# A one-core decoder step: page numbers kept for two loads, and a few orders at its seams

## The chip, the cores and the metric

The kernel is one program on one core of a Trainium2 chip. The metric is the device time in microseconds. The times of before are three runs with a median of 1844.89 us (1842.65 to 1846.63). One more execution was taken by the hardware profiler; every row of the profile below is of that one.

Engines are named as in the profile: PE is the matrix engine (PEld its weight loads), DVE the vector engine, ACT the scalar engine, POOL the general one, and SP the engine whose queue (SPq) issues almost all DMAs here. Each takes its instructions in the order of its own queue.

## The reference, cut to what matters

One layer of a decoder for two groups of requests: a prompt of 1024 tokens and 8 decode requests with 4 new tokens each. The change touches three pieces.

- The prompt's causal attention: 8 heads, scores of queries and keys, exponential, values (`masked_attend` in blocks of 128).
- The decode requests' attention over a paged cache. For each request `pages = page_table[b]` picks 32 pages of 128 tokens; a page holds latents (`cache_ckv`, 256 wide) and rope keys (`cache_kpe`, 32 wide). Keys come from the latents, `k = rms_norm(concat(c @ w_uk, pe))` per head, and `o = softmax(q k) v` runs over 4096 cached tokens and the new ones.
- Keys and values of 256 memory tokens: `k = rms_norm(hm @ w_mk)`, `v = hm @ w_mv`, with `hm = rms_norm(mem)`. They do not depend on the two attentions.

After these come an output projection, memory attention and a gated convolution network; they are left as they are.

## The kernel before

Every product of 32-bit numbers is three matmuls on a high and a low part of each operand (`mm3`, L180; the matmul itself is L185). A high part is cast by ACT or POOL (L197, L201), a low part is left to DVE (L198, L204). The stages in order of time: `phase1`, `phase2a` (the prompt's attention, about 200 to 400 us), `phase2b` (the decode requests, about 400 to 900 us, with `mem_kv` at its end), then `mixed`, `out_proj`, `mem_attention`, `ffn`.

**Who sets the order.** Inside `manual_schedule(engines=...)` the engines named keep the order of the Python program. All other engines, and all of them outside, are ordered by a planner that plays the program forward in modelled time and takes, on each engine, the earliest instruction in the program that it holds to be ready. So in `phase2a` and most of `phase2b` the orders of PE, ACT, DVE and POOL are written by hand and SP's is planned; at the end of `phase2b` only SP's is by hand and the others' are planned. `behind(a, b)` puts instruction a behind b on their engine without a semaphore.

**`phase2a`.** `order` lists 16 units (head h, half G of the queries). A unit has steps; in each step t the loop does: transposes of probabilities `u["T"]` (L993, copied out by ACT L995), pending exponentials `u["e"]` (ACT L985), scores of a coming unit `u["a"]` (PE L185 into tile s of two buffers, drained by DVE L976 and L980 into pr with the row maximum, L982), values `u["V"]` (L1008), and then whatever `extra[t]` holds: key and query transposes of a coming head (`preps`, L946), norms of the keys (`norm`, DVE L922), projected values (`v1`), sums of weights (`weight_sums`, SP L828 and L840, POOL L836 to L839), and one step of each running generator. `jobs[t]` says which scores of which unit fall into step t. One generator is `mix`, with `mix_steps`: four squares with row sums (ACT L1610), a root (DVE), four scalings (ACT L1616), four groups of transposes (PE L1624, copied by DVE L1625). Another is `sample`, which ends in `pages_ahead`: the page table and the latents of quads 0 to 2.

**`phase2b`.** A quad is 4 pages of a request: 8 quads each, 64 in all. `quad_load` reads the four page numbers into registers of SP (L1302, `values_load`), and issues for each page one DMA of transposed latents into tile cT (L1315, three buffers) or of rows into tile ck (L1319, 15 buffers), or both; each call reads the numbers anew. `quad_rot` makes rotated rope keys krq (POOL L1332 to L1334) from cT; `quad_prep` splits cT into ch (ACT L1343) and cl (half on POOL, half on DVE, L1347); `quad_sums` takes squares of the rope keys from ck (ACT L1355, DVE L1356). The steps n count pairs of blocks, two pairs to a quad; `pair_score` does rope scores of the next quad on odd n (PE L1362, copied by ACT L1365) and 24 matmuls (L185) into tile s (two buffers) and s2, whose squares ACT takes (L1384, L1387) and DVE reduces (L1390). Values `quad_pv` (L1460, L1462) follow 20 steps later, after a request's `batch_softmax`, whose parts are numbered r. In part 11 PE spreads a maximum over the partitions (L1448), ACT copies it (L1450), DVE or POOL subtracts it (L1451); the last part is the exponential (ACT L1453).

The loads of the first quads do not all have the same place: cT of quads 0 to 2 is loaded in `phase2a`, of 3 and 4 at n = -1 and 1, ck of quads 0 to 4 at n = 1, 2, 3, 3, 5, and from quad 5 on `quad_load` does both at n = 2Q - 6.

**The end of `phase2b`.** The last request's softmax and values run beside `mem_kv`. Its value products come in four parts, `values(0)`, `(2)`, `(4)`, `(6)`, each 12 matmuls into two accumulators (L185, tile v). Then ACT scales each accumulator into tile vf, which has one buffer (L1592), and issues its DMA to the output (L1593). The norm of the keys uses diag (DVE L1582) and PE L1583.

Of the kernel before, what the change touches and what calls it, by code (L numbers as in the profile page):

```python
# [13 lines left out]
P = 128  # L14
# [140 lines left out]
class Net:  # L155
# [23 lines left out]
    def mm3(self, out, a, b, first=True, last=True):  # L179

        seq = []
        for (ah, al), (bh, bl) in zip(a, b):
            seq += [(ah, bh), (ah, bl), (al, bh)]
        for i, (l, r) in enumerate(seq):
            self.nc.tensor.matmul(out, l, r, start=first and i == 0, stop=last and i == len(seq) - 1)  # L185

    def behind(self, a, b):

# [466 lines left out]
    def phase2a(self):  # L655
# [67 lines left out]

        for n in range(1, len(units)):
            places = {(1, 0): (0, 0, 1, 2), (0, 1): (-1, -1, 0, 1), (0, 0): (0, 0, 1, 1), (1, 1): (0, 1, 1, 2)}
            at = places[order[n - 1][1], order[n][1]] if n > 1 else (0, 0, 1, 1)
            for e in range(4):
                jobs[starts[n - 1] + at[e]].append((units[n], e))

# [3 lines left out]
        for h in range(2, 8):  # L733
            b = 7 * (h - 1)
            put(preps[h], {3: (9, 10, 12, 13), 5: (28, 29, 34, 35), 6: (32, 33, 41, 42), 7: (39, 38, 44, 46)}.get(h, (b, b + 1, b + 3, b + 4)))
        extra[1][:0] = preps[0][2:]
        spread(late[0][0], 11, 21)
        spread(late[1][0], 14, 24)
        spread(late[0][1], 22, 27)
        spread(late[1][1], 25, 30)  # L740
        spread(late[2][0], 24, 30)
        sums = [(i, z) for i in (NK, NK + 1, *range(NK)) for z in range(2)]
        times = (0, 1, 3, 4, 5, 7, 8, 9, 11, 12, 14, 15, 16, 25, 26, 27, 29, 30, 36, 37, 39, 40, 41, 43, 44, 46)
        for t, x in zip(times, sums):
            extra[t].append(lambda x=x: self.weight_sums(half(), *x))

# [17 lines left out]
        with tc.manual_schedule(engines={E.PE, E.Activation, E.DVE, E.Pool}):  # L764
            for f in preps[0][0], preps[0][1], v1[0], preps[1][0], preps[1][1]:
                f()
            for e in range(4):
                units[0]["a"](e)
                if e:
                    units[0]["e"](e - 1)  # L770
                    if e % 2:
                        v1[e // 2 + 1]()
            units[0]["e"](3)
            for f in norm[:2]:
                f()
            v1[3]()
            extra[0][:0] = norm[2:]
            steps, outs, pend, V = [], {}, [], []
            self.lows = []
            t = 0  # L780
            for n, u in enumerate(units):
                for k, banks in enumerate(u["steps"]):
                    self.flush()
                    for b in banks:
                        u["T"](b)
                    for f in outs.pop(t, []):
                        f()
                    for f in pend:
                        f()
                    pend = []  # L790
                    for w, e in jobs[t]:
                        w["a"](e)
                        pend.append(lambda w=w, e=e: w["e"](e))
                    self.flush()
                    for f in V:
                        f()
                    V = [lambda u=u, b=b: u["V"](b) for b in banks]
                    if k == len(u["steps"]) - 1:
                        outs.setdefault(t + 2, []).append(u["copy"])
                        outs.setdefault(t + 3, []).append(u["out"])  # L800
                        if order[n] == (7, 0):
                            outs[t + 3].append(lambda: steps.append(mix()))
                    for f in extra[t]:
                        f()
                    t += 1
                    if t == 32:
                        steps.append(sample())
                    steps = [x for x in steps if next(x, 0) is None]
            self.flush()
            self.lows = None  # L810
            for fs in [V] + [outs[t] for t in sorted(outs)] + [[]] * 4:
# [306 lines left out]
    def pages_ahead(self):  # L1118

        nc, I = self.nc, self.I  # L1120
        pc = self.pc3 = self.open("p3c", side="right")
        self.pages = self.t(pc, [1, NB * NPG], I32, "pages")
        nc.sync.dma_start(self.pages, I["pages"])
        self.cosT, self.sinT = (self.t(pc, [P, 8, P], F32, x) for x in ("cosT", "sinT"))
        nc.sync.dma_start(self.cosT, I["c_cosT"])
        nc.sync.dma_start(self.sinT, I["c_sinT"])
        yield
        self.quads = {Q: self.quad_load(None, Q) for Q in range(3)}
        yield
        nc.vector.tensor_scalar(self.cosT, self.cosT, self.col("gk_rep"), None, ALU.mult)  # L1130
        yield
        nc.vector.tensor_scalar(self.sinT, self.sinT, self.col("gk_perm"), None, ALU.mult)


    def phase2b(self):
# [19 lines left out]
        def at(n, pos, f, *a):  # L1155
            ev.setdefault((n, pos), []).append(lambda: f(*a))
# [45 lines left out]
                    at(n + k, pos, f)  # L1202
        E = mybir.EngineType

        raws = []

        def steps(n0, n1):
            for n in range(n0, n1):
                Q, v = n // 2, n - 16 - LAG
                if n >= 4 and n % 2 == 0 and Q + AHEAD < NB * 8:  # L1210
                    quads[Q + AHEAD] = self.quad_load(p, Q + AHEAD)
                for k, dst, src in ((2, b4, self.b_dram), (16, self.fold4, I["c_fold4"]), (64, wuv, I["w_uv"])):
                    if n == k:
# [19 lines left out]
                run(n, 1)  # L1233
# [60 lines left out]
        for w, q in ((self.w2h, self.qah), (self.w2l, self.qal)):  # L1294
            nc.scalar.copy(w[:, :, d], q[:, :, b].rearrange("p k h t -> p k (h t)"))

    def quad_load(self, p, Q, d=None):

        nc, I = self.nc, self.I
        new = d is None  # L1300
        d = d or {}
        ld, rvs = nc.values_load_multi_w_load_instructions(  # L1302
            self.pages[0:1, Q * 4 : Q * 4 + 4], engines=[mybir.EngineType.SP], min_val=0, max_val=319
        )
# [1 line left out]
        if len(self.page_dma) >= 5:  # L1306
            for x in ld:
                self.tc.add_manual_dep(
                    x.ins, self.page_dma[-5].ins.name,
                    mybir.DependencyInfo(mybir.DependencyClass.NoSync, mybir.DependencyReason.DATA), reason="registers",  # L1310
                )
        dmas = []
        if new:
            cT = d["cT"] = self.t(self.pc3, [P, 4, 320], F32, "cT", 3)
# [79 lines left out]
    def batch_softmax(self, p, pp, s, r, final):  # L1394
# [50 lines left out]
            nc.vector.tensor_scalar(s["dg"], self.ident[:32, :32], mm, None, ALU.mult)  # L1445
        elif r == 11:
            bc = self.t(pp, [P, 512], F32, "m", 1)[:, :32]
            nc.tensor.matmul(bc, self.ones[:32], s["dg"], start=True, stop=True)  # L1448
            s["bc"] = self.t(p, [P, 32], F32, "bc", 2)
            nc.scalar.copy(s["bc"], bc)  # L1450
            (nc.vector if final else nc.gpsimd).tensor_tensor(S, S, s["bc"].unsqueeze(1).broadcast_to([P, 33, 32]), ALU.subtract)  # L1451
        else:
            nc.scalar.activation(S, S, AF.Exp, scale=SCALE)  # L1453

    def quad_pv(self, pp, Q, d, s):

# [47 lines left out]
    def mem_kv(self, raws, wk0):  # L1504
# [44 lines left out]
        def values(k):  # L1549
            wh, wl = (x.rearrange("p k n -> p (k n)").rearrange("p (k n) -> p k n", k=2) for x in self.stream(I["w_mv"][k // 2], 8))  # L1550
            for i in range(2):
                t = slice(i * P, i * P + P)
                self.mm3(av[i], [tuple(x[:, t] for x in xs[k + e]) for e in range(2)],
                         [(wh[:, e], wl[:, e]) for e in range(2)], first=k == 0, last=k == 6)

        values(0)
        yield
# [31 lines left out]
        values(6)  # L1589
        for i in range(2):  # L1590
            vf = self.t(p, [P, 512], F32, "vf")
            nc.scalar.activation(vf, av[i], AF.Copy, scale=rt[:, i : i + 1])  # L1592
            nc.scalar.dma_start(O["o_mv"][i * P : i * P + P], vf)  # L1593
        self.close("pskv")
        self.close("pkv")
# [840 lines left out]
```

## Time and profile before

| | us |
|---|---|
| median of three runs | 1844.89 |
| the profiled execution | 1842.78 |
| its span, first to last instruction | 1841.1 |
| PE busy in it | 1807.4 |
| POOL, ACT, DVE busy | 699.7, 925.4, 1350.2 |

The span leaves out 1.7 us around it. PE's idle time is the span less its busy time; an idle gap carries in brackets what ended it. In a list of waits the numbers are: us in total, times, longest. In a table of windows each engine has its busy us and in brackets its instructions; PEclk is the granted clock of PE as a share of full speed. A slowed PE counts as busy.

### The profile page before, as it was taken

The numbers are of one execution on the slowest core, as the hardware profiler recorded it, in microseconds if no ns is written. First come the engines' busy times: TensorE is split into PE (matmuls) and PEld (weight loads), VectorE is DVE, ScalarE is ACT, GpSimd is POOL, SyncE is SP. The second block draws the span as 40 slices with busy tenths as digits, with TensorE's granted clock in tenths as the row PEclk, the third lists the DMA queues.
The fourth block names the chain that finished last, engine by engine and source line by source line (L and its number), as shares of the span: only waits on it lengthen the run. The fifth ranks groups of instructions, "written<-read, shape, count | busy, mean of one in ns | idle before, by whom it ended". The sixth has DMA issues, their size and how long they took to land.

```text
span 1841.1 us, 39335 instructions
## 1 busy us (share of the span) xinstructions
PE 1807.4 (98%) x14222; PEld 1705.8 (93%) x14222; DVE 1350.2 (73%) x2805; ACT 925.4 (50%) x1916; POOL 699.7 (38%) x852
## 2 busy tenths in 40 slices
PE   9999999999999999999899999999999999999999
PEld 8999777679999999998799979999999999999999
DVE  7855767656778766776545666998888888878664
ACT  7435676766656555555433556533333333444442
POOL 1021555533544454454123110377766777400000
PEclk9999999999999999999999999999999999999999
DMA  8101363557766666654555255322222222495242
GB/s 320 47 25 65 104 205 105 185 174 201 226 188 195 188 182 184 184 166 144 158 154 178 73 179 161 107 82 70 94 82 70 73 80 76 142 328 171 80 152 77
DMA packets 153188, 261.19 MB, mean 142 GB/s; under 512 B 20897, under 2 KB 97538, under 8 KB 152994
## 3 DMA queue, kind: packets, MB, share of 16 engines
q1 hardware_dynamic: 152130, 257.63, 45.3%
q8 instruction: 112, 1.84, 0.4%
q10 hardware_dynamic: 864, 1.05, 0.2%
q14 instruction: 82, 0.67, 0.1%
HBM read 212.79 MB, written 45.82 MB: 140 GB/s over the span
## 4 chain that ended last, share of the span: by engine, by line
PE 71%; issue 5%; DVE 4%; SPq 3%; DMA 2%; POOL 2%; ACT 2%; POOLq 0%; DVEq 0%; ACTq 0%
PE s L185 14%; PE d L185 12%; PE b L185 8%; PE F L185 7%; PE X L185 7%; PE E L185 7%; PE A L185 3%; PE y L185 3%; SPq L1315 2%; PE o L1008 2%; PE tp L993 1%; PE tp L185 1%; PE o L1462 1%; DMA cT<-cT 1%; POOL cl L1347 1%
## 5 line engine op out<-in xcount | busy, mean ns | idle before, releaser
L185 PE MATMUL s<-w2h,ch 128*128 128x288 f32 (+1 forms) x1024 | 304.4, 297 | 0.5 <-ACT S L1365 0.5
L185 PE MATMUL s<-w2h,cl 128*128 128x288 f32 (+1 forms) x1024 | 296.3, 289 | 2.3 <-POOL cl L1347 2.3
L185 PE MATMUL s<-w2l,ch 128*128 128x288 f32 (+1 forms) x1024 | 295.2, 288 | 0.0
L185 PEld LDWEIGHTS s<-w2h,ch 128*128 128x128 f32 x1024 | 193.2, 189 | 9.0 <-issue 2.5
L185 PEld LDWEIGHTS s<-w2h,cl 128*128 128x128 f32 x1024 | 192.9, 188 | 4.1 <-POOL cl L1347 3.9
L185 PEld LDWEIGHTS s<-w2l,ch 128*128 128x128 f32 x1024 | 193.4, 189 | 0.0
L1390 DVE TENSOR_REDUCE ss<-sq 128x16 f32<-128x1024 f32 x128 | 155.4, 1214 | 33.0 <-ACT sq L1387 32.7
L1347 POOL TENSOR_TENSOR cl<-cT,ch 128x512 fp32r<-128x512 f32 x64 | 82.9, 1295 | 120.4 <-ACT ch L1343 115.4
L1387 ACT ACTIVATE sq<-s 128x512 f32<-128x512 f32 x128 | 76.7, 599 | 88.3 <-PE s L185 88.2
L1384 ACT ACTIVATE sq<-s 128x512 f32<-128x512 f32 x128 | 76.9, 601 | 73.3 <-PE s L185 70.9
L197 ACT CAST a<-brb 128x528 fp32r<-128x528 f32 x77 | 49.0, 636 | 109.5 <-PE d L185 105.8
L185 PE MATMUL d<-a,w 128*128 128x264 f32 x768 | 95.2, 284 | 0.0
L185 PEld LDWEIGHTS d<-a,w 128*128 128x128 f32 x768 | 94.3, 188 | 0.0
L198 DVE TENSOR_TENSOR a<-brb,a 128x528 fp32r<-128x528 f32 x77 | 54.4, 707 | 52.8 <-ACT a L197 52.7
L2072 POOL TENSOR_TENSOR lo<-s,hi 128x1024 fp32r<-128x1024 f32 x20 | 64.0, 3200 | 45.7 <-ACT hi L2071 45.7
L185 PE MATMUL mm<-whi,xh 128*128 128x256 f32 (+3 forms) x272 | 77.1, 285 | 0.0
L185 PE MATMUL mm<-wlo,xh 128*128 128x256 f32 (+3 forms) x272 | 76.9, 285 | 0.1
L185 PE MATMUL mm<-whi,xl 128*128 128x256 f32 (+3 forms) x272 | 76.9, 286 | 0.0
L2127 ACT COPY a<-A 128x264 f32<-128x264 f32 x43 | 16.2, 376 | 120.5 <-PE A L185 114.2
L1386 DVE TENSOR_TENSOR S<-s,S 128x64 f32<-128x64 f32 x128 | 28.1, 219 | 63.6 <-ACT sq L1384 63.6
L1343 ACT CAST ch<-cT 128x512 fp32r<-128x512 f32 x128 | 73.6, 628 | 2.0 <-DMA cT<-cT 1.3
L2193 POOL TENSOR_TENSOR cv<-cv,row 128x1056 f32<-128x1056 f32 x22 | 65.1, 2960 | 21.0 <-ACT cv L2192 21.0
(746 smaller groups left out, 6397.1 us busy)
## 6 DMA issues: line engine op xcount, KB each, us to landing
cT<-cT SPq DMA_DIRECT2D x256, 160.0 KB, 2.7
ck<-ck SPq DMA_DIRECT2D x256, 144.0 KB, 3.4
raw<-w_up SPq DMA_DIRECT2D x44, 512.0 KB, 3.6
wsumd<-wsum SPq DMA_DIRECT2D x26, 512.0 KB, 3.4
actd<-cv SPq DMA_DIRECT2D x44, 264.0 KB, 2.4
brb<-actd SPq DMA_DIRECT2D x44, 264.0 KB, 5.9
wsum<-w_down SPq DMA_DIRECT2D x22, 512.0 KB, 3.6
raw<-wsumd SPq DMA_DIRECT2D x20, 512.0 KB, 3.8
```

Of the source, the lines that this page charges most:

```text
L185: self.nc.tensor.matmul(out, l, r, start=first and i == 0, stop=last and i == len(seq) - 1)
L197: first = {"act": nc.scalar.copy, "pool": nc.gpsimd.tensor_copy, "dve": nc.vector.tensor_copy}[eng](hi, src)
L198: low = lambda: nc.vector.tensor_tensor(lo, src, hi, ALU.subtract)
L1008: nc.tensor.matmul(u["o"][g : g + 64, o : o + m * P], s["v"][:, j, h % 4], th[:, z * P : (z + m) * P], start=j == 0, stop=b == len(banks) - 1,
L1315: dmas.append([nc.sync.dma_start(cT[:, j], I["cT"][bass.ds(rv, 1)].rearrange("a p n -> (a p) n")) for j, rv in enumerate(rvs)])
L1343: nc.scalar.copy(d["h"][:, k], src[k])
L1347: (nc.vector if k else nc.gpsimd).tensor_tensor(d["l"][:, k], src[k], d["h"][:, k], ALU.subtract)
L1384: nc.scalar.activation(sq[:, 0], ps[:, :, n0 : n0 + 256], AF.Square)
L1387: nc.scalar.activation(sq[:, 1], pt.rearrange("p (e d) -> p e d", e=2), AF.Square)
L1390: yield lambda: nc.vector.tensor_reduce(s["ss"][:, g0 : g0 + 2].rearrange("p e (z h) -> p z e h", z=2), sq.rearrange("p z e (h d) -> p z e ...
L2072: eng.tensor_tensor(lo, src, hi, ALU.subtract)
L2193: nc.gpsimd.tensor_tensor(cv, cv, row, ALU.mult)
```

## The change

- `quad_pages` is split off from `quad_load`; page numbers that were read are kept in `rvs` and passed to the second load of the same quad. Those of quads 3 and 4 are read at the end of `pages_ahead`.
- In `phase2b` the first loads get other steps: cT of quads 5 to 7 at n = 3, 5, 7, ck of quads 0 to 7 at n = 1, 3, 4, 5, 6, 3, 8, 8; loads of both from quad 8 on. `quad_sums` of quads 0 to 4 moves to n = 6, 8, 10, 10, 11 (before 4, 6, 8, 7, 9).
- Tiles m, o and s2 are allocated before s, so that their places in PSUM (PE's output banks) are given in that order.
- In `phase2a`: v1's last part and the second half of head 0's transposes move from ahead of step 0 and from step 1 to steps 1 and 2; the third unit's scores move to steps 3, 3, 3, 4 (before 2, 2, 3, 4); the first two `weight_sums` move one step on; `mix` does one square in its first step and three in its second (before two and two).
- At the end: the first matmul of `values(6)` is put behind L1448 on PE, and the second vf behind the last exponential on ACT.

```diff
     def mm3(...):
+        returns its first matmul (head)
...
-            at = places[order[n - 1][1], order[n][1]] if n > 1 else (0, 0, 1, 1)
+            at = {1: (0, 0, 1, 1), 2: (0, 0, 0, 1)}.get(n) or places[order[n - 1][1], order[n][1]]
...
-        extra[1][:0] = preps[0][2:]
+        extra[2][:0] = preps[0][2:]
...
-        times = (0, 1, 3, 4, 5, 7, 8, 9, 11, 12, 14, 15, 16, 25, 26, 27, 29, 30, 36, 37, 39, 40, 41, 43, 44, 46)
+        times = (1, 2, 3, 4, 5, 7, 8, 9, 11, 12, 14, 15, 16, 25, 26, 27, 29, 30, 36, 37, 39, 40, 41, 43, 44, 46)
...
-                if k not in (0, 2, 8):
+                if k not in (1, 2, 8):
                     yield
...
-            v1[3]()
             extra[0][:0] = norm[2:]
+            extra[1][:0] = v1[3:]
...
         self.quads = {Q: self.quad_load(None, Q) for Q in range(3)}
+        self.rvs = {Q: self.quad_pages(Q) for Q in (3, 4)}
...
         ppt, pp = self.open("ps3t", space=PSUM), self.open("ps3", space=PSUM)
+        for tag in ("m", "o"):
+            self.t(ppt, [P, 512], F32, tag, 1)
+        self.t(pp, [P, 512], F32, "s2", 2)
...
-                if n >= 4 and n % 2 == 0 and Q + AHEAD < NB * 8:
+                if n >= 10 and n % 2 == 0 and Q + AHEAD < NB * 8:
                     quads[Q + AHEAD] = self.quad_load(p, Q + AHEAD)
...
-                    at(n + (6 if Q < 2 else 3), 0, self.quad_sums, Q + 1, quads[Q + 1], st[(Q + 1) // 8])
+                    at((6, 8, 10, 10, 11)[Q + 1] if Q < 4 else n + 3, 0, self.quad_sums, Q + 1, quads[Q + 1], st[(Q + 1) // 8])
...
-                if n in (-1, 1):
-                    quads[Q + 4] = self.quad_load(None, Q + 4)
-                for k in {1: (0,), 2: (1,), 3: (2, 3), 5: (4,)}.get(n, ()):
-                    self.quad_load(p, k, quads[k])
+                if n in (-1, 1, 3, 5, 7):
+                    k = Q + 4
+                    rvs[k] = rvs.get(k) or self.quad_pages(k)
+                    quads[k] = self.quad_load(None, k, None, rvs[k])
+                for k in {1: (0,), 3: (5, 1), 4: (2,), 5: (3,), 6: (4,), 8: (6, 7)}.get(n, ()):
+                    self.quad_load(p, k, quads[k], rvs.get(k))
...
-    def quad_load(self, p, Q, d=None):
+    def quad_load(self, p, Q, d=None, rvs=None):
+        rvs = rvs or self.quad_pages(Q)
...
-            nc.tensor.matmul(bc, self.ones[:32], s["dg"], start=True, stop=True)
+            self.spread = nc.tensor.matmul(bc, self.ones[:32], s["dg"], start=True, stop=True)
...
-            nc.scalar.activation(S, S, AF.Exp, scale=SCALE)
+            self.exp = nc.scalar.activation(S, S, AF.Exp, scale=SCALE)
...
+                if k == 6 and i == 0:
+                    self.behind(x, self.spread)
...
+            if i:
+                self.behind(x, self.exp)
```

More of the change, by code (lines that the diff above doesn't have):

```diff
@@ L184, in mm3 @@
         for i, (l, r) in enumerate(seq):
-            self.nc.tensor.matmul(out, l, r, start=first and i == 0, stop=last and i == len(seq) - 1)
+            x = self.nc.tensor.matmul(out, l, r, start=first and i == 0, stop=last and i == len(seq) - 1)
+            if i == 0:
+                head = x
+        return head
     def behind(self, a, b):
@@ L1203, in phase2b @@
         E = mybir.EngineType
-        raws = []
+        raws, rvs = [], self.rvs
         def steps(n0, n1):
@@ L1295, in batch_enter, with quad_pages @@
             nc.scalar.copy(w[:, :, d], q[:, :, b].rearrange("p k h t -> p k (h t)"))
-    def quad_load(self, p, Q, d=None):
-        nc, I = self.nc, self.I
-        new = d is None
-        d = d or {}
+    def quad_pages(self, Q):
+        nc = self.nc
         ld, rvs = nc.values_load_multi_w_load_instructions(
@@ L1311, in quad_load @@
                 )
+        return rvs
+    def quad_load(self, p, Q, d=None, rvs=None):
+        nc, I = self.nc, self.I
+        new = d is None
+        d = d or {}
+        rvs = rvs or self.quad_pages(Q)
         dmas = []
@@ L1552, in values @@
                 t = slice(i * P, i * P + P)
-                self.mm3(av[i], [tuple(x[:, t] for x in xs[k + e]) for e in range(2)],
-                         [(wh[:, e], wl[:, e]) for e in range(2)], first=k == 0, last=k == 6)
+                x = self.mm3(av[i], [tuple(x[:, t] for x in xs[k + e]) for e in range(2)],
+                             [(wh[:, e], wl[:, e]) for e in range(2)], first=k == 0, last=k == 6)
+                if k == 6 and i == 0:
+                    self.behind(x, self.spread)
         values(0)
@@ L1591, in mem_kv @@
             vf = self.t(p, [P, 512], F32, "vf")
-            nc.scalar.activation(vf, av[i], AF.Copy, scale=rt[:, i : i + 1])
+            x = nc.scalar.activation(vf, av[i], AF.Copy, scale=rt[:, i : i + 1])
+            if i:
+                self.behind(x, self.exp)
             nc.scalar.dma_start(O["o_mv"][i * P : i * P + P], vf)
```

## The prediction, made before the result was known

> **What bounds the kernel now.** I read the page first, then PE's list of waits, then the timelines around each wait.
>
> ```profile
> span 1841.1 us, 39335 instructions
> PE 1807.4 (98%) x14222; PEld 1705.8 (93%) x14222; DVE 1350.2 (73%) x2805; ACT 925.4 (50%) x1916; POOL 699.7 (38%) x852
> ```
>
> PE is idle for 33.7 us of the span. The change removes no matmul, so it can win only idle time and time at a lowered clock.
>
> ```profile
> PE o L1460 <- ACT S L1453: 5.3, 1, 5.3
> PE s L1362 <- POOL krq L1334: 5.1, 3, 2.3
> PE tp L946 <- DVE k L922: 1.8, 2, 1.1
> ```
>
> These three groups are 12.2 us, and all lie at places that the change edits: the last exponential, the first quads of `phase2b`, and head 0's keys at the opening of `phase2a`. A gap can cost more than itself. The table of windows (us; PE, PEld, DVE, ACT, POOL busy and instructions; granted clock; DMA share; GB/s) has these rows:
>
> ```profile
> 214.00:219.00 5.00, 4.98 (x17) 3.56 (x17) 2.68 (x10) 0.58 (x2) 2.21 (x4) 0.50 0.52 169
> 431.00:434.00 3.00, 1.58 (x12) 1.58 (x13) 1.03 (x2) 2.41 (x7) 2.54 (x4) 1.00 0.78 209
> 441.00:445.00 4.00, 3.73 (x18) 3.73 (x19) 2.81 (x4) 2.55 (x6) 1.45 (x2) 0.57 0.79 220
> 894.00:901.00 7.00, 6.51 (x71) 5.69 (x71) 0.02 (x1) 3.27 (x7) 0.00 (x0) 0.68 0.19 60
> ```
>
> After the 5.3 us gap the clock is 0.68 for 7 us: 2.2 us lost. At 441 it is 0.57 for 4 us: 1.7 us lost. At 431 it stays at 1.00.
>
> **The change, 1: page numbers and first loads.** PE's three waits for rope keys, what held POOL before the second and third, and SP's queue:
>
> ```profile
> 402.40 0.46 PE L1362 MATMUL s<-bd,krq 128*128 128x128 f32 x2 [1.41 <-POOL krq L1334]
> 432.42 0.49 PE L1362 MATMUL s<-bd,krq 128*128 128x128 f32 x2 [1.43 <-POOL krq L1334]
> 441.27 0.80 PE L1362 MATMUL s<-bd,krq 128*128 128x128 f32 x2 [2.29 <-POOL krq L1334]
> ```
>
> ```profile
> 430.96 0.46 POOL L1332 TENSOR_TENSOR krq<-cT,cosT 128x128 f32<-128x128 f32 x1 [5.78 <-DMA cT<-cT]
> 439.82 0.45 POOL L1332 TENSOR_TENSOR krq<-cT,cosT 128x128 f32<-128x128 f32 x1 [6.21 <-DMA cT<-cT]
> ```
>
> ```profile
> 414.95 8.60 SPq L1319 DMA_DIRECT2D ck<-ck  x12
> ...
> 425.25 1.92 SPq L1315 DMA_DIRECT2D cT<-cT  x4
> ...
> 434.64 2.23 SPq L1315 DMA_DIRECT2D cT<-cT  x4
> ...
> 446.34 2.33 SPq L1315 DMA_DIRECT2D cT<-cT  x4
> ```
>
> The latents of quads 5, 6 and 8 are issued at 425.25, 434.64 and 446.34. The first two were late: POOL stood idle for them, PE for POOL. SP was never idle there; its price is in the chain (start, us) and the landing times on the page:
>
> ```profile
> 406.12 6.05 PE s L185 x48
> ...
> 429.25 0.30 SPq L1302
> ...
> 430.78 0.32 SPq L1319
> ```
>
> ```profile
> cT<-cT SPq DMA_DIRECT2D x256, 160.0 KB, 2.7
> ck<-ck SPq DMA_DIRECT2D x256, 144.0 KB, 3.4
> ```
>
> One read of four page numbers takes 1.5 us (429.25 to 430.78), four issues about 2.1, and PE needs 3.1 us for a pair (6.05 for 48 matmuls, and the rope).
>
> Quad 5: before, SP did ahead of its latents two loads of latents, four of rows and seven reads. After, it does two, one, and two reads (the numbers of 3 and 4 are read in `phase2a`: 3 us more in SP's queue there, with only stores and loads of weight sums behind them, which no PE wait names). That is 3 x 2.1 + 5 x 1.5 = 13.8 us less, 411.5 for the issue. But the tile is that of quad 2, still read until 412.8:
>
> ```profile
> 402.17 0.69 DVE L1347 TENSOR_TENSOR cl<-cT,ch 128x512 fp32r<-128x512 f32 x1
> ...
> 411.79 1.02 DVE L1347 TENSOR_TENSOR cl<-cT,ch 128x512 fp32r<-128x512 f32 x1
> ```
>
> So the issue is at 412.8 to 414.9, landing at 417.5; PE asks for the keys at 431. Quad 6: two loads and four reads less, 10.3 us, of which 2.3 go to waits for tiles (1 us for quad 4's, 1.3 for quad 5's): issue at 426.6, landing 431.3, keys (1.4 us of POOL) 432.7; PE asks at 402.5 + 11 x 3.1 = 437. Quad 8: four reads less, 3.8 us net: issue 442.5, landing 447.3, keys 448.7; PE asks at 402.5 + 15 x 3.1 = 449. That is the thinnest cover, 0.3 us (1 us where the opening transposes come between). What is late next, if any, is here. The rows of quads 1 to 4 are now loaded 3 to 6 us later, and their `quad_sums` stand in ACT's queue ahead of the squares that free s. By the same count rows 3 land at 434 and are asked for at n = 10, 434: ACT waits some tenths, and s has two buffers, so PE feels a delay only beyond about one pair (3.1 us).
>
> Won: 1.43 + 2.29 + 1.7 of clock = **5.4 us**. Its ends: 0 if the latents stay where they were in SP's order, 5.4.
>
> [...] The row at 441, 0.57 right behind that gap, speaks for the gap as the cause, and the row at 431 for a bound between 1.43 and 2.29.
>
> **2: the first pair.** Allocating m, o and s2 first gives tile s other banks than those that `mix` copied out just before 402.40; if that copy, not the keys, ended the wait, PE starts up to 1.41 earlier. But the sixth matmul of the pair reads the half of cl that DVE ends at 402.86 (row above), 0.4 us before it runs now. I take **0.35**; the ends are 0 and 1.41.
>
> **3: mix.** ACT's second square stands ahead of an exponential that PE waits for:
>
> ```profile
> 388.84 0.63 ACT L1610 ACTIVATE k<-b_all 128x512 f32<-128x512 f32 x1
> ```
>
> ```profile
> 391.11 0.76 PE L993 MATMUL tp<-ident,pr 128*128 128x128 f32 x5 [1.09 <-ACT pr L985]
> ```
>
> It moves behind it: the gap shrinks by 0.7. The three squares then end when the second two did, and the copies behind them hold PE by 0.4. I take **0.3** (0 to 0.7).
>
> **4: the opening.** The waits for L922 are 1.12 and 0.65. Beside them:
>
> ```profile
> 205.76 0.33 PE L993 MATMUL tp<-ident,pr 128*128 128x128 f32 x1 [0.60 <-ACT pr L985]
> ...
> 212.87 0.63 PE L185 MATMUL s<-kTh,qTh 96*128 96x320 f32 x1 [0.60 <-ACT qTh L201]
> ```
>
> ```profile
> 211.78 0.68 DVE L976 CUSTOM_DVE_ANT_0 pr<-s,cmask 128x512 f32<-128x512 f32 x1
> ```
>
> Part v1 (six matmuls, 0.7 us) no longer covers the first wait, 0.60 to 1.3, but with the values of the next bank (0.9 us) it fills those for L922. Then the new places bite: the casts of head 0's second half (0.6 and 0.7 on ACT) now stand behind two exponentials, of which the second waits for the maximum that DVE ends at 212.7. It ends at 213.6, the casts at 214.9, and the scores start 2 us later than now. In exchange the values and transposes that now run at 217.5 to 219.4, on half clock (row 214), are done by then. DVE then bounds the three score blocks, at 1.6 us each; the third starts at 218.5 instead of 219.46. I take **0.9**. The ends: -1.0 (the clock stays half for another window), +2.4 (no half clock at all). The moved `weight_sums` keep their order on POOL: nothing.
>
> **5: the end.** PE runs `values(4)` and `(6)` at 0.24 us a matmul, then L1448; then ACT and DVE:
>
> ```profile
> 883.16 4.32 PE v L185 x18
> ```
>
> ```profile
> 884.45 0.22 DVE L1445 TENSOR_SCALAR dg<-ident,mm 32x32 f32<-32x32 f32 x1
> ...
> 889.72 1.26 DVE L1451 TENSOR_TENSOR S<-S,bc 128x1056 f32<-128x1056 f32 x1 [0.61 <-ACT bc L1450]
> ```
>
> ```profile
> 888.80 0.40 PE L1448 MATMUL m<-dg,ones 32*128 32x32 f32 x2
> ```
>
> ```profile
> 887.50 0.69 ACT L1592 ACTIVATE vf<-v,rt 128x512 f32<-128x512 f32 x1 [0.35 <-PE v L185]
> 888.23 1.23 ACTq L1593 DMA_DIRECT2D o_mv<-vf  x1
> 889.50 0.19 ACT L1450 COPY bc<-m 128x32 f32<-128x32 f32 x1 [1.30 <-PE m L1448]
> 892.78 0.69 ACT L1592 ACTIVATE vf<-v,rt 128x512 f32<-128x512 f32 x1 [3.09 <-DMA o_mv<-vf]
> 893.36 1.07 ACT L1453 ACTIVATE S<-S 128x1056 f32<-128x1056 f32 x1
> ```
>
> The input of L1448 is ready at 884.7, but twelve matmuls of `values(6)` run first. And the second vf, waiting for the one buffer, holds the exponential from 891.0 (end of L1451) to 893.4. After: `values(4)` ends at 885.9, L1448 at 886.3, `values(6)` (cover for what follows) at 889.2; copy 886.5, subtraction 887.8, exponential 888.9. If ACT takes the first vf and its DMA issue (0.7 + 1.2) ahead of the exponential, as it now takes them ahead of the copy, it ends at 890.7. I take that: PE goes on 3.8 us earlier than 894.5, after a gap of 1.5 us, which by the row at 431 keeps the clock: 2.2 more, **6.0**. The ends: 2.4 (only the second vf gives way, the low clock stays), 7.5 (exponential ahead of the first vf). The second vf then waits behind the exponential for its buffer; the splits that follow on ACT wait for PE's values anyway.
>
> **Sum:** 5.4 + 0.35 + 0.3 + 0.9 + 6.0 = 13.0 us. The profiled execution took 1842.8, so 1829.8 of its kind; the median of the runs is 2.1 above it, and 1844.9 - 13.0 = **1832**.
>
> **Rivals.**
> (a) *The low clock does not follow from these gaps*: both dips stay, 1.7 + 2.2 less: 1836. For it: by 214 the clock had fallen after gaps of 1.1 us at most (the L922 row). Against: the dips sit right behind the two longest gaps. [...]
> (b) *SP's order stays*: the planner, not the program, places SP's loads; if it keeps the rows ahead of latents 5 and 6, part 1 gives nothing: 1837. Against: the order before was the program's.
> (c) *The end gives only its lower end*, the exponential freed but L1448 late: 3.6 less, 1835.5.
> (d) *Slower: late rows.* The row loads of quads 0 to 4 come behind a latents load that waits for its tile on SP; each then lands late for its `quad_sums`, ACT stops, s fills up, PE stops. The price of one is that of the wait at 441, 4.0 us; five are 20, against 13 won: 1852. It decides from a delay of about one pair plus 2.3, 5.4 us beyond my count, for each. Against: my count leaves tenths to 3 us at each.
>
> **How the numbers follow.** Forecast 0.55, (a) 0.10, (b) 0.13, (c) 0.08, (d) 0.07, and 0.07 that several terms fail and 0 to 4 us are left. A measurement here tells about 0.2%, 3.7 us, from no change: faster by more 0.85, within 0.08, slower 0.07. The range is 1827 (all upper ends, 17.4) to 1841; it leaves out (d) and the failure of several terms.
>
> **What would show it.** Part 1: no gaps at L1362 from quad 5 on, clock 1.00 there, latents 5 on SP by 415. Part 2: the gap at the first L1362 under 1. Part 5: L1448 ahead of `values(6)`, exponential ahead of the second vf, the gap at L1460 under 2. Part 4: the third unit's third block earlier by about 1. It is wrong if ACT waits for ck, if L1362 waits at quad 8, or if new gaps stand in the planned stages after 905.

## The result, and the profile after

| | before | changed |
|---|---|---|
| median, us | 1844.85 (1841.99 to 1848.18, 15 runs) | 1842.09 (1840.25 to 1844.61, 15 runs) |
| ratio, 95% interval | | 0.9986 (0.9979 to 0.9993) |
| profiled execution, us | 1842.78 | 1843.82 |

The change is worth about 2.6 us (1.3 to 3.9); forecast were 13. Two executions of the kernels below, 1948.96 and 3069.06 us long, were slow ones, and all ratios are of the others. The profiled execution of the changed kernel is one of its longer ones and that of before one of its shorter ones, so the two spans stand in the wrong order by a microsecond. Stages can be compared, the spans can't. The page of the changed kernel:

```profile
span 1842.1 us, 39314 instructions
PE 1809.4 (98%) x14222; PEld 1706.1 (93%) x14222; DVE 1354.1 (74%) x2805; ACT 922.9 (50%) x1916; POOL 697.1 (38%) x852
```

PE is idle for 32.7 us; it was 33.7. Its list of waits in the changed kernel (us in total, times, longest):

```profile
PE tp L996 <- ACT pr L988: 4.2, 8, 0.9
PE s L185 <- DVE pr L983: 4.1, 6, 1.8
PE o L1475 <- ACT S L1468: 2.3, 1, 2.3
PE s L185 <- POOL cl L1362: 2.3, 7, 0.5
PE s L1377 <- POOL krq L1349: 2.3, 2, 1.8
PE A L2044 <- DVE hr L246: 1.8, 1, 1.8
```

Lines have moved by 3 to 19: L1362 for cl was L1347, L1377 was L1362, L1475 was L1460. Three groups of waits that the change aimed at did shrink: for the last exponential 5.3 to 2.3, for rope keys 5.1 to 2.3, and those for L922 (now L925) are gone from the list. But three waits of 1.8 us each are new: for pr in the opening, for rope keys at quad 8, and for hr in the network after 905. The clock gave nothing back. Table of windows of the changed kernel (us; PE, PEld, DVE, ACT, POOL busy and instructions; clock; DMA share; GB/s), cut at the instants where the clock changes:

```profile
211.60:215.01 3.41, 1.65 (x7) 0.96 (x8) 1.56 (x3) 2.66 (x7) 3.10 (x6) 1.00 0.45 153
215.01:218.43 3.42, 3.42 (x12) 2.93 (x11) 2.25 (x8) 0.00 (x0) 0.55 (x1) 0.50 0.43 137
218.43:221.84 3.41, 3.41 (x14) 2.31 (x14) 1.97 (x8) 0.00 (x0) 0.39 (x1) 0.50 0.62 195
232.08:235.49 3.41, 1.59 (x9) 1.10 (x7) 3.16 (x11) 1.92 (x5) 2.40 (x4) 1.00 0.46 152
235.49:238.91 3.42, 3.42 (x13) 1.60 (x11) 2.58 (x11) 0.00 (x0) 2.29 (x4) 0.50 0.50 174
453.95:457.36 3.41, 1.62 (x13) 1.38 (x13) 2.98 (x7) 2.32 (x5) 2.36 (x4) 1.00 0.57 154
457.36:460.77 3.41, 3.41 (x17) 3.41 (x16) 3.41 (x4) 0.60 (x1) 3.33 (x5) 0.50 0.88 254
880.61:884.03 3.42, 2.60 (x22) 2.37 (x20) 3.04 (x5) 1.70 (x2) 0.31 (x2) 1.00 0.22 34
884.03:887.44 3.41, 3.41 (x11) 2.73 (x11) 3.13 (x13) 0.00 (x0) 0.00 (x0) 0.50 0.71 237
894.27:897.68 3.41, 3.30 (x32) 3.06 (x36) 0.82 (x4) 2.40 (x6) 0.00 (x0) 0.50 0.25 91
1167.33:1170.75 3.42, 2.74 (x23) 2.52 (x21) 3.31 (x10) 1.05 (x1) 0.33 (x2) 1.00 0.00 0
1170.75:1174.16 3.41, 2.25 (x17) 2.11 (x18) 2.02 (x8) 0.66 (x2) 0.00 (x0) 1.00 0.52 159
```

Six windows of 3.41 us at half clock: 20.5 us. The trace of before has six as well; one of them was at 441.07 and two behind the gap at the end (891.63 to 898.46), where the prediction saw them. The dips moved and did not become fewer.

### The profile page after: what moved, and what is told of

Read it like the earlier page. It is cut to its first block, busy times and chain, and to the rows that moved or that the text cites. A ratio compares the mean times of both kernels' runs of the same rounds, so it can differ in the third digit from the quotient of the medians.

```text
span 1842.1 us, 39314 instructions
## 1 busy us (share of the span) xinstructions
PE 1809.4 (98%) x14222; PEld 1706.1 (93%) x14222; DVE 1354.1 (74%) x2805; ACT 922.9 (50%) x1916; POOL 697.1 (38%) x852
## 3 DMA queue, kind: packets, MB, share of 16 engines
q8 instruction: 112, 1.84, 0.4%
## 4 chain that ended last, share of the span: by engine, by line
PE 73%; DVE 5%; issue 4%; ACT 2%; POOL 2%; DMA 1%; SPq 1%; DVEq 0%; POOLq 0%; ACTq 0%
PE s L185 16%; PE d L185 12%; PE b L185 8%; PE F L185 7%; PE E L185 7%; PE X L185 7%; PE A L185 3%; PE y L185 2%; PE o L1011 2%; PE tp L996 1%; PE tp L185 1%; PE o L1477 1%; PE tp L949 1%; PE t L185 1%; ACT pr L988 1%
## 5 line engine op out<-in xcount | busy, mean ns | idle before, releaser
L1362 POOL TENSOR_TENSOR cl<-cT,ch 128x512 fp32r<-128x512 f32 x64 | 83.8, 1310 | 126.7 <-ACT ch L1358 118.0
L185 PE MATMUL d<-a,hi 128*128 128x264 f32 x552 | 72.0, 284 | 0.0
```

The source lines that it names most:

```text
L185: x = self.nc.tensor.matmul(out, l, r, start=first and i == 0, stop=last and i == len(seq) - 1)
L1362: (nc.vector if k else nc.gpsimd).tensor_tensor(d["l"][:, k], src[k], d["h"][:, k], ALU.subtract)
```

## The experiments

Each was timed beside the kernel before; us are (ratio - 1) x 1844.5.

| kernel | ratio (95%) | us |
|---|---|---|
| opening alone | 1.0013 (1.0004 to 1.0022) | +2.4 |
| loads alone | 0.9980 (0.9971 to 0.9990) | -3.7 |
| end alone | 0.9984 (0.9975 to 0.9993) | -3.0 |
| all but the opening | 0.9956 (0.9943 to 0.9968) | -8.1 |
| third unit's scores alone | 0.9999 (0.9990 to 1.0008) | -0.2 |
| mix and places alone | 0.9998 (0.9989 to 1.0007) | -0.4 |
| all but the opening, both accumulators | 0.9953 (0.9940 to 0.9966) | -8.7 |
| the same, latents 8 ahead of rows 7 | 0.9952 (0.9939 to 0.9965) | -8.9 |
| changed, without sum 5 | 0.9977 (0.9968 to 0.9987) | -4.2 |
| before, without sum 5 | 1.0001 (0.9991 to 1.0012) | +0.2 |
| spread alone | 0.9979 (0.9968 to 0.9990) | -3.9 |
| exponential alone | 0.9990 (0.9980 to 0.9999) | -1.8 |
| changed, v1 back | 0.9992 (0.9983 to 1.0000) | -1.5 |
| loads and end | 0.9975 (0.9966 to 0.9985) | -4.6 |

**The opening alone.**

```diff
+ before, with: at = {..., 2: (0, 0, 0, 1)}; extra[2][:0] = preps[0][2:]; extra[1][:0] = v1[3:]; times = (1, 2, 3, ...
```

> The kernel before with the edits of phase2a's opening alone (third unit's scores at steps 3, 3, 3, 4, head 0's second half of transposes and v1's last part one step later, first two weight_sums one step later). Theory 1, the opening is what ate the gain: PE's scores and exponentials wait for each other there, 1.5 to 2 us of new gaps between 200 and 240, and the rest of the kernel is as before: 2 to 4 us slower than the kernel before (ratio 1.001 to 1.002). The prediction's own term: 0.9 us faster. Rival, the loss in the profile of the changed kernel was one execution's low clock only: within 1 us of no change, and the gaps between 200 and 240 sum to the 4.1 us of before.

It is slower by 2.4 (0.7 to 4.1): the term that the prediction counted as a gain of 0.9 is a loss.

**The loads alone.**

```diff
+ before, with quad_pages, rvs, and the new steps of cT, ck and quad_sums
```

> The kernel before with the page numbers kept and the new steps of the first loads and quad_sums alone. Theory 1, SP's queue was late in the changed kernel because phase2a ended 3 us later: here SP starts on the latents at 403 as before, quad 8's are issued near 445, its keys make PE wait under 0.5 us, both old waits (1.43 and 2.29) are gone: 3.5 to 5 us faster. Rival, the queue of SP is full by itself and the wait only moves to quad 8: a wait of 1.5 to 2 us stays at its rope matmul, 1 to 2.5 us faster.

A gain of 3.7, and a wait of 2.42 at quad 8 although SP began at 402.83, as early as before. So the late hand-over is not what makes quad 8 late: the theory fell here. The rival, a full queue, foresaw the wait, but later traces speak against it as well (step 1 below).

**The end alone.**

```diff
+ before, with behind(x, self.spread) at k == 6, i == 0, and behind(vf, self.exp) for the second vf
```

> The kernel before with the two orders at the end alone (values(6) behind the spread matmul, second vf behind the last exponential). Theory 1, only the first of the two accumulators is held behind the spread, so six matmuls (1.4 us) still run ahead of it: the spread comes after 18 matmuls and not after 12, the gap ahead of the last values is 2.3 us and not 1.5: 2 to 4 us faster (the 3.0 us of the gap, and up to 1.7 of clock). The prediction's term: 6.0. Rival, this part gives nothing because the following stage waits for something else: within 1 us.

3.0 (1.3 to 4.6), gap 2.3: as theory 1 said.

**All but the opening.**

```diff
+ changed, with the three pieces of the opening as before
```

> The changed kernel with phase2a's opening put back as before; everything else changed. Theory 1 (opening costs 3 us and makes SP late): 5 to 8 us faster than the kernel before, and 3 to 5 faster than the changed kernel; no wait over 0.5 us at quad 8. Rival (the opening costs nothing, the wins are small by themselves): 2 to 3.5 us faster than before, as the changed kernel.

8.1: the opening costs the changed kernel about 5 us, twice what it costs alone. In the traces the opening's stage itself, 196 to 250, is worse by 3.4: PE is idle for 6.25 us in place of 4.59, and three windows and not two run at half clock. PE's wait at quad 8 in the kernel without the new opening, and POOL ahead of it:

```profile
455.37 0.40 PE L185 MATMUL s<-w2h,cl 128*128 128x288 f32 x1 [1.32 <-POOL cl L1362]
```

```profile
448.89 0.46 POOL L1349 TENSOR_TENSOR krq<-krq,krq 128x128 f32<-128x128 f32 x1
452.01 2.08 POOL L1423 TENSOR_TENSOR S<-S,ss 128x768 f32<-128x768 f32 x1 [2.66 <-DVE ss L246]
```

The keys of quad 8 are ready in time (PE takes them at 450.36 without a wait); the next late thing is POOL's first step of the first softmax, which waits for DVE and stands ahead of cl.

**The third unit's scores alone**, to find the part of the opening that costs.

```diff
+ before, with: at = {..., 2: (0, 0, 0, 1)}
```

> The kernel before with one line of the opening alone: the third unit's scores at steps 3, 3, 3, 4 instead of 2, 2, 3, 4; transposes, v1's last part and weight_sums stay. Theory 1: it is this line that costs, because three score blocks, their drains on DVE and their exponentials on ACT now come in one step, and PE has nothing between them: 1 to 2.5 us slower, a wait for DVE's pr of about 1.5 us and waits of transposes for ACT's pr appear, as in the whole opening alone. Rival, the moved transposes and v1 cost: within 0.8 us of no change here.

No change, and no such waits: it is not this line alone.

**Mix and places.**

```diff
+ before, with: if k not in (1, 2, 8); m, o and s2 allocated first
```

> The kernel before with mix's square moved (one in the first step, three in the second) and m, o, s2 allocated ahead of s, nothing else. The prediction's terms: 0.3 and 0.35 (ends 0 and 2.1): 0.65 us faster. Theory now, from the changed kernel without the opening, which won 8.1 where loads and end alone won 3.4 and 3.0: 1 to 2 us faster, the first rope matmul of phase2b waits under 0.3 us for its place or keys instead of 1.41. Rival: within 0.4 us, the 1.4 us are an interaction with the loads.

0.4 (a gain of 2.0 to a loss of 1.3). In its trace the first pair waits 1.0 for cl in place of 1.41 for the keys, which is the prediction's 0.35; the "1 to 2" expected here was wrong.

**Both accumulators behind the spread.**

```diff
-                if k == 6 and i == 0:
+                if k == 6:
```

> The changed kernel with the old opening, and the first matmul of both accumulators of values(6) behind the spread matmul (the change holds only the first accumulator's). Theory: the spread runs after 12 matmuls and not 18, 1.4 us earlier; twelve matmuls and not six are left to cover copy, subtraction and exponential: the gap of 2.3 us ahead of the last values falls to about 1, so 1 to 1.5 us faster than the changed kernel with the old opening, 3 where a low clock goes with it. Rival: the exponential waits for ACT's first vf, which itself waits for the later end of the first accumulator, so the gap stays at 2 or more and the time within 0.5 us.

The end of the changed kernel, then of this one:

```profile
890.06 0.40 PE L1463 MATMUL m<-dg,ones 32*128 32x32 f32 x2
894.38 0.64 PE L1475 MATMUL o<-cn,S 128*32 128x257 f32 x1 [2.31 <-ACT S L1468]
...
894.99 5.09 PE L1477 MATMUL o<-ck,S 128*32 128x257 f32 x61
```

```profile
884.40 0.57 PE L1463 MATMUL m<-dg,ones 32*128 32x32 f32 x2
889.15 0.40 PE L1475 MATMUL o<-cn,S 128*32 128x257 f32 x1 [1.18 <-ACT S L1468]
...
889.58 3.66 PE L1477 MATMUL o<-ck,S 128*32 128x257 f32 x61
```

In the changed kernel six matmuls of `values(6)` (0.24 us each) run behind the spread, here all twelve, and the gap falls from 2.31 to 1.18. The 61 last matmuls take 1.4 us less: in the changed kernel 2.69 us of them lie in the window at 0.50 that ends at 897.68, which is 1.35 lost, and the three rows ahead of them take 0.64 to 0.65 us, here 0.38 to 0.42. But that can't be put down to this edit: in the trace of all but the opening, whose end is that of the changed kernel, they also take 3.66 behind a gap of 2.31. So the rows show 1.1 us; the medians (8.1 and 8.7) differ by less than their intervals can tell.

**Latents of quad 8 ahead of the rows of 7.**

```diff
+ at n == 10: pages and cT of quad 8, then ck of 7, then ck of 8; at n == 8 only ck of 6
```

> As the kernel with both accumulators behind the spread, and the latents of quad 8 issued ahead of the rows of quad 7 (pages of quad 8 are read first, then its latents, rows of 7, rows of 8). Theory, the queue in front of quad 8's latents is what made them late: they are issued 1.8 us earlier and land 2 or more earlier, no wait at the rope matmul of quad 8; 0 to 1.5 us faster than without. Rival: rows of quad 7 are then late for quad_sums, ACT stops ahead of the casts of ch, PE waits for cl or s: 0.5 to 2 us slower.

The same time: with the old opening the keys of 8 were not what ended the wait (cl was, 1.6 us in this trace). This and the kernel before it, five executions each, are the best versions tried, both faster than before and than the changed kernel.

**The collision.** The changed kernel's opening on DVE, POOL and PE, then the same on DVE and POOL in the kernel before:

```profile
231.71 0.59 DVE L904 TENSOR_TENSOR hr<-hr,sq_tok 32x4 f32<-32x4 f32 x1
...
232.41 0.71 DVE L232 TENSOR_SCALAR rqx<-hr 32x8 f32<-32x8 f32 x1
...
233.35 0.58 DVE L234 TENSOR_SCALAR rqy<-rqy 32x8 int32<-32x8 int32 x1
```

```profile
231.56 0.73 POOL L839 TENSOR_TENSOR wsum<-wsum 128x256 f32<-128x256 f32 x1 [3.80 <-DMA wsum<-w_down]
232.37 0.73 POOL L840 TENSOR_TENSOR wsum<-wsum 128x256 f32<-128x256 f32 x1
233.18 0.73 POOL L841 TENSOR_TENSOR wsum<-wsum 128x256 f32<-128x256 f32 x1
```

```profile
234.84 0.47 PE L185 MATMUL s<-kTh,qTh 96*128 96x448 f32 x1 [1.82 <-DVE pr L983]
```

```profile
231.23 0.15 DVE L901 TENSOR_TENSOR hr<-hr,sq_tok 32x4 f32<-32x4 f32 x1
...
231.87 0.16 DVE L231 TENSOR_SCALAR rqy<-rqy 32x8 int32<-32x8 int32 x1
```

```profile
232.60 0.73 POOL L836 TENSOR_TENSOR wsum<-wsum 128x256 f32<-128x256 f32 x1 [3.81 <-DMA wsum<-w_down]
```

POOL's additions (the fifth sum of weights) begin when a DMA lands, at a time of their own. DVE's steps follow PE and ACT. Before, they end 0.6 us ahead of POOL; in the changed kernel they come later against POOL, and three of them take 0.6 to 0.7 instead of 0.15. Each of the three ends with the addition that runs beside it: at 232.30, 233.12 and 233.93, the additions at 232.29, 233.10 and 233.91. The drains behind them are 1.4 late, and PE waits 1.82. The next two kernels leave the four additions of this sum out, and with them a part of the computation:

```diff
         sub = nc.gpsimd.tensor_tensor
+        if (i, z) != (0, 0):
-        sub(a22, a21, a22, ALU.add)  (and three more)
+            sub(a22, a21, a22, ALU.add)  (and three more)
```

> The changed kernel without POOL's four additions of the fifth of the 26 sums of weights (its load and its store stay; this part of the computation is left out). Theory 2, a collision: the new opening brings DVE's small steps for the norm (0.15 us each) about 1 us later against POOL's additions, they overlap, the small steps take 0.6 to 0.7 us, the drain of pr ends 1.5 us late, PE waits 1.8 us at 233 and the window behind it runs at half clock. Then here: small steps at 0.15 us again, no wait over 0.6 us for pr there, no low clock at 235, 2.5 to 4 us faster than the changed kernel, 5 to 7 faster than before. Rival, DVE is late for its own queue (more drains in a row after the moved scores): the wait of 1.5 to 1.8 stays, time as the changed kernel within 1 us.

> Control: the kernel before without the same four additions (this part of the computation is left out). Theory 2: there the small steps end before POOL begins, so nothing is gained, within 1 us of the kernel before. Rival, the additions cost something by themselves (POOL, the store or DVE's other work): over 2 us faster.

Without the additions the steps are short again, at the same place in DVE's order, and the low clock at 235 is gone (from 235.10 on the matmuls of 448 columns take 0.36 to 0.47 us there, where in the changed kernel the one at 235.62 takes 0.74):

```profile
232.61 0.15 DVE L905 TENSOR_TENSOR hr<-hr,sq_tok 32x4 f32<-32x4 f32 x1
232.87 0.16 DVE L232 TENSOR_SCALAR rqx<-hr 32x8 f32<-32x8 f32 x1
233.26 0.16 DVE L234 TENSOR_SCALAR rqy<-rqy 32x8 int32<-32x8 int32 x1
```

The wait falls to 0.4, and the control gains nothing, so the collision is shown, by the rows. Between 196 and 250 its absence is worth 3.1 in the traces: PE is idle for 4.81 us (6.25 with the additions, 4.49 in the kernel before), and two windows run at half clock (three; two). In the median its price is smaller than expected and not certain: 4.2 (2.4 to 5.9) against 2.6, 1.6 and not 2.5 to 4. How hard the two meet differs from one execution to the next: with the additions present, the three traces with the new opening (the changed kernel, the opening alone, v1 back) have a wait of 1.5 to 1.9 for pr; of eleven with the old order or the scores' line alone three have one of 0.8 to 1.3.

**The two orders at the end, one by one.**

```diff
+ before, with behind(x, self.spread) only      | before, with behind(vf, self.exp) only
```

> The kernel before with only the first matmul of values(6) put behind the spread. Theory: the exponential is still held behind the second vf by the output DMA that vf's one buffer waits for, so the earlier spread gives nothing, within 1 us. Rival: the second vf comes behind the exponential anyway, 2 to 3 us faster, as both orders together.

> The kernel before with only the second vf put behind the last exponential. Theory: this is the part that gives the gain of the two; the gap ahead of the last values falls from 5.3 (3.1 where the output DMA lands early) to 2.5 to 3.0: 1 to 3 us faster. Rival: nothing alone, since the spread is late.

The first expectation was wrong: the spread alone gives 3.9 (1.8 to 5.9), as much as both orders within the intervals. ACT in that kernel:

```profile
891.13 0.69 ACT L1597 ACTIVATE vf<-v,rt 128x512 f32<-128x512 f32 x1 [1.41 <-PE v L185]
...
892.27 1.08 ACT L1456 ACTIVATE S<-S 128x1056 f32<-128x1056 f32 x1 [0.45 <-DVE rqh L245]
894.00 0.69 ACT L1597 ACTIVATE vf<-v,rt 128x512 f32<-128x512 f32 x1 [0.65 <-DMA o_mv<-vf]
```

With the spread early, the planner puts the exponential ahead of the second vf by itself; the second order changes nothing then, and alone it gives 1.8 (0.2 to 3.7).

**v1 back, and the loads with the end.**

```diff
+ changed, with v1[3]() ahead of step 0     | before, with the loads and the end
```

> The changed kernel with v1's last part back ahead of step 0 (and the second half of the norm in step 0 behind it, as in the changed kernel); the other edits of the opening stay. Theory 2 (the opening costs by making DVE late by about 1 us, so that its small steps meet POOL's additions): the six matmuls cover the first wait for pr again (0.6 instead of 0.9 and 0.2), but the later waits for the second half's casts stay; if DVE's small steps then still come after POOL's start the wait of 1.8 stays and the time is that of the changed kernel within 1.5 us; if they come ahead of it, 2.5 to 4 us faster than the changed kernel. Rival (v1's place is the whole loss): 5 us faster than the changed kernel, as with the old opening.

> The kernel before with the loads and the end, without the opening, mix and the places in PSUM. Theory: the parts add up: 6.5 to 7 us faster than before (3.7 and 3.0 alone); a wait of 1.5 to 2.5 at quad 8's rope keys is left, as in the loads alone. Rival: the places in PSUM and mix are what lets SP start earlier and so take that wait away in the changed kernel with the old opening; then 8 us here would speak against it, and 6.5 or less for it.

v1's place is not it: 1.5 faster than before, as the changed kernel within the intervals, and the collision's wait is 1.9. Loads and end give 4.6 (2.8 to 6.3), less than 6.7 but within the intervals; no wait at quad 8's keys is left there, 1.27 for cl instead, so that wait does not hang on mix or places either. Up to the end this kernel is the loads alone, with the same order on SP and PE at quad 8, and there the wait was 2.42: it comes and goes from one execution to the next.

## Why the prediction was wrong, point by point

Measured alone, the terms are 3.7 + 0.4 + 3.0 - 2.4 = 4.7, against 5.4 + 0.35 + 0.3 + 6.0 + 0.9 = 13.0; in the changed kernel another 1.4 goes in a place that no term had, which leaves 3.3 where 2.6 was measured.

- **Step 4 had the wrong sign, a loss of 2.4 alone for a gain of 0.9; it is the step that failed.** "The moved `weight_sums` keep their order on POOL: nothing" and the end "-1.0" looked at POOL's order and not at its time against DVE's. The third block of the third unit's scores does start earlier from the first scores, as forecast (18.8 us after them, before 19.6), but on half clock (0.50; its matmuls take 0.57 to 0.64 us, before 0.36 to 0.45); ACT's waits replace DVE's, DVE's steps come 1.5 us later against POOL's (231.23 and 232.60 before, 231.71 and 231.56 now), and the collision makes PE wait 1.82 (0.41 without the additions), with a third window at half clock behind it. Without the additions the opening's stage costs about what it cost before, so in these traces the collision is most of the loss there. The medians leave more open: without sum 5 the kernel is still 3.9 us slower than all but the opening, and the rows name 1.4 of it (the wait at L2044, below). Which of the moved pieces makes DVE late stays open: neither the scores alone nor v1 alone.
- **Step 5 was mis-sized, 3.0 for 6.0.** "`values(4)` ends at 885.9, L1448 at 886.3" took the order to hold all twelve matmuls; it names the first of accumulator 0 only, and the planner ran the six of accumulator 1 first. So the spread came after 18 matmuls, and the gap is 2.3 and not 1.5. Of the 2.2 for the clock little came back: PE worked 4.0 us at half clock behind the gap (894.49 to 898.46), and in the changed kernel 3.3 (894.38 to 897.68). That is 3.0 for the gap and 0.3 for the clock at most. The 5.3 to win from is not in every execution either: in the six traces whose end is that of before, the gap is 4.9 to 5.3 in four and 3.1 in two. The output DMA held the second vf for 2.7 to 3.4 us in the four, and for 1.15 and 1.19 in the two, here the kernel with the loads alone:

```profile
890.57 0.69 ACT L1601 ACTIVATE vf<-v,rt 128x512 f32<-128x512 f32 x1 [1.19 <-DMA o_mv<-vf]
```

- **Step 1 was nearly right, 3.7 for 5.4.** The waits at quads 5 and 6 went. "The thinnest cover, 0.3 us" at quad 8 was the one that broke. The group of SP's reads from 403 to the issue of quad 8's latents, in the kernel before and in the changed one, and SP's issues in the latter:

```profile
L1302 SPq TENSOR_LOAD <-pages x9: 295/298/304, 406.9 to 444.7; - x9
```

```profile
L1309 SPq TENSOR_LOAD <-pages x7: 296/298/303, 409.2 to 446.8; - x7
```

```profile
417.65 1.91 SPq L1330 DMA_DIRECT2D cT<-cT  x4
...
430.93 1.92 SPq L1330 DMA_DIRECT2D cT<-cT  x4
...
448.43 1.93 SPq L1330 DMA_DIRECT2D cT<-cT  x4
```

Two reads (3 us) are saved and not four: the planner had already taken the first reads of quads 3 and 4 ahead. SP began its loads 3.1 later (406.14 for 403.00), and quad 8 is issued at 448.43 and not at 442.5. But the late issue did not make the wait. POOL's first step for the keys of quad 8, in the changed kernel and in all but the opening:

```profile
454.93 0.61 POOL L1347 TENSOR_TENSOR krq<-cT,cosT 128x128 f32<-128x128 f32 x1 [5.84 <-DMA cT<-cT]
```

```profile
447.82 0.46 POOL L1347 TENSOR_TENSOR krq<-cT,cosT 128x128 f32<-128x128 f32 x1 [4.14 <-DMA cT<-cT]
```

The last of the four DMAs landed 4.8 us after its issue in the changed kernel and 5.4 in the loads alone, the two traces with this wait. In the five others with the same order on SP it took 2.8 to 3.5, and none has the wait, though v1 back began as late (406.26) and issued quad 8 at 448.25. What made the two DMAs land late stays open. Nor would an earlier landing have won it all: where the keys come in time, PE waits 1.0 to 1.6 for cl, behind POOL's softmax step.
- **Steps 2 and 3** (0.65) fit the 0.4 measured.
- **The clock.** 3.9 of the 13.0 were to come from dips that follow a long gap. Rival (a) was nearer in result, but the length of a gap did not decide it: behind the gap of 1.82 us that ends at 234.84 the clock fell to 0.50, behind that of 1.84 that ends at 1171.90 it stayed at 1.00. PE's busy time in windows of 3.41 us, as the last section shows, says more.
- **New, as the last list of the prediction feared:** a wait in a planned stage after 905. The changed kernel, then all but the opening:

```profile
1169.79 0.28 PE L185 MATMUL X<-b211h,hi 128*128 128x264 f32 x1
1171.90 1.48 PE L2044 MATMUL A<-ident,hr 128*128 128x128 f32 x10 [1.84 <-DVE hr L246]
```

```profile
1169.34 0.28 PE L185 MATMUL E<-b221h,hi 128*128 128x264 f32 x1
1169.46 1.37 PE L2044 MATMUL A<-ident,hr 128*128 128x128 f32 x10
```

PE takes L2044 behind the first matmul on b211h in place of the first on b221h, 36 matmuls earlier, ahead of its input: 1.8 where 0.4 was lost in the stage. The kernel before has it at the later place too. Only the three traces with the new opening and everything else (the changed kernel, the one without sum 5, v1 back) have the early place; the opening alone has the later one. That the planner's model ranks it so because the opening moved its modelled times is argued; it was not tried.

Rivals (b) and (d) did not come: SP took the order of the program, and no row was late enough for ACT to stop. The first pair's gap for the keys is gone as Part 2 asked (1.0 for cl stands in its place), and latents 5 came 2.7 later than the 415 given.

## What to carry to other kernels

When a step is moved, hold its new time against work that runs by another clock: a chain that DMAs release does not move with it (here DVE's steps came 0.48 us later and POOL's additions 1.04 earlier), and the 1.5 us between them brought the two engines together. An order on one matmul binds one accumulator; name the first of each. Price a gap by the windows of 3.41 us that it falls into (one of 1.8 us cost nothing more in the changed kernel, and two windows at 0.50 in v1 back), and a stall that hangs on one DMA's landing, 2.8 to 5.4 us after its issue at quad 8, by more than one execution.

## What the runs showed of the hardware

**The clock goes by windows of 3.41 us.** In all sixteen traces (both kernels and fourteen experiments) low stretches begin at multiples of 3.413 us from each other within one execution; in that of before they begin at 212.38, 441.07, 864.33 and 891.63, which are 67, 124 and 8 of them apart. In the table above PE is busy 1.59 to 1.65 of 3.41 us in the three windows at 211.60, 232.08 and 453.95, and each next one is at half clock (0.50); behind 2.25 and 2.74, which share the gap of 1.84 that ends at 1171.90, it stays at 1.00. In the trace of v1 back that gap fell into one window, and two windows followed at half clock:

```profile
1167.01:1170.42 3.41, 1.58 (x13) 1.37 (x13) 3.31 (x11) 0.32 (x1) 0.00 (x0) 1.00 0.28 62
1170.42:1173.83 3.41, 3.41 (x15) 3.15 (x16) 1.22 (x2) 0.71 (x2) 0.00 (x0) 0.50 0.24 96
1173.83:1177.25 3.42, 3.42 (x17) 3.42 (x17) 0.47 (x1) 1.55 (x2) 0.19 (x1) 0.50 0.00 0
```

Over the sixteen traces, 36 of 38 full-clock windows with PE busy under half were followed by one at half clock; from 0.5 to 0.7 it went both ways (10 of 62). In the two of before and of the changed kernel it was seven of seven under half (0.98 to 1.65 us busy) and none of seven from 0.5 to 0.7 (1.97 to 2.35). Twelve fuller windows of the sixteen traces were followed by one too: in before that at 860.91, with PE busy for 3.27. Nine of the twelve have PE busy for about 0.75 and stand at the place of 880.61 above (2.60 us), where 16 of the 22 matmuls have one column. So busy time is not the whole rule. But where a gap falls in the windows, which differs from one execution to the next, has a part: the same gap of 1.8 us cost nothing more in the changed kernel, and in v1 back two windows at 0.50, which is 3.4 us.

**DVE beside POOL.** DVE steps of 0.15 us took 0.58 to 0.71 while POOL's additions of 0.73 ran, and ended with them. Not every step was held: a reciprocal (L1019, one input) took 0.15 at 234.19, under the fourth addition (233.99 to 234.71). Two of the three that were held (L232, 0.71, and L234, 0.58) read one tensor only as well; what tells them from the reciprocal, no run here shows.
